# A two-layer trunk with a mixture of experts: the second layer's out projection taken tile by tile, late rows normed on VectorE, low weight parts behind the overflow branch

## The chip, the cores and the metric

The kernel runs on one core of one Trainium2 chip. The metric is the device time of one launch in microseconds; lower is better. TensorE (PE) multiplies matrices, VectorE (DVE) and ScalarE (ACT) do elementwise work, GpSimd (POOL) does elementwise work and issues the indirect (gathering) DMAs, SyncE (SP) issues the other DMAs.

## The reference

512 rows of 1024 numbers pass two layers. Layer 0 mixes by a chunked causal gMLP, layer 1 by dilated attention (three dilation groups of four heads); beside the mixer each layer attends to a memory of 256 rows. Then each layer does the same:

```
att = concat([mix, mo], -1) @ w_out            # out projection
x = layer_norm(ALPHA * x + att, ln1_g, ln1_b)
expert, gate = route(h, w_router, b_router)    # softmax, best group of 4 experts, top 2 in it
ffn = moe_ffn(h, expert, gate, w_gate, w_up, w_down)   # (silu(x@wg) * (x@wu)) @ wd
x = layer_norm(ALPHA * x + ffn, ln2_g, ln2_b)
```

All is float32; there are 16 experts with three 1024x1024 matrices each.

## The kernel before

The 512 rows lie in four tiles of 128 (t = 0 to 3), the 1024 columns in two halves of 512. A float32 product is made of three fp32r products: each operand is split into a high part (`wh`, `xh`, `ah`; ScalarE's cast) and a low part (`wl`, `xl`, `al`; VectorE's subtraction), and TensorE adds wh*xh, wl*xh and wh*xl.

**Recording and order.** The program is written once in Python and a scheduling layer of the framework sets the order on each engine, except in the expert stage, where the kernel's own generators do it (their helper is line 68). An engine's queue is in order: an instruction that waits holds all behind it.

**Out projection and first norm** (`out_proj_ln1`). The weights `woutb` are split one 128x1024 chunk of two half rows at a time, the tiles are taken in two pairs, and each pair splits all chunks again. For each (tile, half) the products collect in the PSUM tile `att`; VectorE adds it to `ALPHA` times the row (`xrows`, L770), takes statistics (L771), TensorE turns the rows (`hTp`), ScalarE copies them (`hT`), and TensorE makes the router's logits from them. Small steps on VectorE (L175 to L180, a Newton iteration for the reciprocal root; L787, L788) fix up the logits into `lg` (L794), so the router doesn't wait for the normed rows. The rows are normed beside: ScalarE (L793), then times `ln_g` (L797) and plus `ln_b` (L798) on GpSimd, with three of the eight L797 on VectorE; then each tile goes to `hbuf` in HBM. In layer 1 the products of the dilated attention's last group of heads (`dsc`, `dpt`, `po`) and the turn of its mix (`mixT`, `catb`) stand ahead; out-projection products are ready for the memory's part of the columns before, and stand between them on TensorE. Layer 0 has a `fill`: the projections of the memory for layer 1 (`pm`, `v`, `kT`), issued in two parts around the routing.

**Routing** (`route`). From `lg` a softmax (L825 to L835, result `pr`), the choice of group and experts, ranks by matmuls, and indices `ix` (L985).

**Experts** (`moe`, `stream`). An indirect DMA on GpSimd gathers the rows of each of the first two experts from `hbuf` by `ix` into `xg`. `gates` makes the gate weights on VectorE. The first three weight chunks are split (`wh` and `wl` from `wexp`). Then every engine reads a number of overflow blocks (`tabi`) and branches: with these inputs there is no overflow, and the branch skips its code (L1254 to L1257). Behind the branch `stream` turns the gathered rows (`xt`), splits them (`xh`, `xl`) and runs gate, up and down products (`pg`, `pu`, `pd`). Its lines in the profile are L68. Memory comes from pools that are opened and closed in order, so a tile of a later pool can lie on that of an earlier one and must wait until its last reader is done.

Of the kernel before, what the change touches and what calls it, by code (L numbers as in the profile page):

```python
# [11 lines left out]
F32 = mybir.dt.float32  # L12
# [5 lines left out]
OP = mybir.AluOpType  # L18
# [56 lines left out]
class Trunk:  # L75
# [106 lines left out]
    def rsqrt(self, pool, var):  # L182
        t = pool.tile([P, 3], F32, tag="rsq", name="rsq", bufs=2)
        list(self.rsqrt_steps(t, var, self.nc.vector))
        return t[:, 0:1]
# [557 lines left out]
    def out_proj_ln1(self, layer, spl, pl, wo, cat, order, xr, g, b, more, buf, fill=None):  # L743
# [6 lines left out]
        for pair in range(2):  # L750
            tiles = (2 * pair, 2 * pair + 1)
            accs = {(t, half): self.acc("att") for half in range(2) for t in tiles}
            st = {t: pl.tile([P, 2, 6], F32, tag="lst", name="lst", bufs=4) for t in tiles}
            hT = {t: pl.tile([P, KT, P], F32, tag="hT", name="hT", bufs=2) for t in tiles}
            for half in range(2):
                nj = nk // 2
                for js in [(j,) for j in range(nj - 2)] + ([(nj - 2, nj - 1)] if pair and half else [(nj - 2,), (nj - 1,)]):
                    parts = {j: self.split(spl, wo[half][:, order[2 * j]:order[2 * j] + 2]) for j in js}
                    for t in tiles:
                        ts = slice(t * P, (t + 1) * P)  # L760
                        for j in js:
                            h, l = parts[j]
                            for i in range(2):
                                c = slice(i * 512, (i + 1) * 512)
                                k = order[2 * j] + i
                                self.mm3(accs[t, half], (cat[k][0][:, ts], cat[k][1][:, ts]), (h[:, c], l[:, c]),
                                         start=(j == 0 and i == 0), stop=(j == nj - 1 and i == 1))
                for t in tiles:
                    z = xr[:, t, half * 512:(half + 1) * 512]
                    nc.vector.scalar_tensor_tensor(z, z, ALPHA, accs[t, half], op0=OP.mult, op1=OP.add)  # L770
                    nc.vector.bn_stats(st[t][:, half], z)  # L771
                    x = self.tp("hTp")
                    for i in range(4):
                        nc.tensor.transpose(x[:, i * P:(i + 1) * P], z[:, i * P:(i + 1) * P], self.ident)
                    nc.scalar.copy(hT[t][:, 4 * half:4 * half + 4].rearrange("p a b -> p (a b)"), x)
            if pair:
                self.early += [self.load_half(layer, *divmod(i, 6)) for i in more]
                if not fill:
                    for t in range(2):
                        nc.sync.dma_start(self.hbuf[t * P:(t + 1) * P, :], xr[:, t])  # L780
                self.table(pl, AF.Exp, lg[:, 1, :1])
            for t in tiles:
                mv = pl.tile([P, 2], F32, tag="lmv", name="lmv", bufs=2)
                nc.vector.bn_aggr(mv, st[t])
                rs = self.rsqrt(pl, mv[:, 1:2])
                sh = pl.tile([P, 1 + NE], F32, tag="lsh", name="lsh", bufs=2)
                nc.vector.scalar_tensor_tensor(sh[:, :1], mv[:, 0:1], -1.0, rs, op0=OP.mult, op1=OP.mult)  # L787
                nc.vector.scalar_tensor_tensor(sh[:, 1:], sums[:, 0], sh[:, :1], sums[:, 1], op0=OP.mult, op1=OP.add)  # L788
                o = lps[t % 2][:, t * NE:(t + 1) * NE]
                for k in range(KT):  # L790
                    last = nc.tensor.matmul(o, hT[t][:, k], gw[:, k], start=(k == 0), stop=(k == KT - 1))
                z = xr[:, t]
                nc.scalar.activation(z, z, AF.Identity, scale=rs, bias=sh[:, :1])  # L793
                nc.vector.scalar_tensor_tensor(lg[:, t], o, rs, sh[:, 1:], op0=OP.mult, op1=OP.add)  # L794
                for half in range(2):
                    v = slice(half * 512, (half + 1) * 512)
                    (nc.vector if t + half > 2 else nc.gpsimd).tensor_mul(z[:, v], z[:, v], g[:, v])  # L797
                nc.gpsimd.tensor_add(z, z, b)  # L798
                if pair or fill:
                    nc.sync.dma_start(self.hbuf[t * P:(t + 1) * P, :], z)  # L800
        if fill:
            with self.tc.issue_after(last.ins):
                fill(0)
        self.route(Carve(buf()), lg)
# [14 lines left out]
    def route(self, pl, lg):  # L819
# [205 lines left out]
    def wh_tile(self, pool):  # L1025
        return pool.tile([P, 1024], F32R, tag="wh", name="wh", bufs=AHEAD_H + 1)
# [90 lines left out]
    def stream(self, layer, px, pool, scat, loaded, chunk, parts):  # L1117
# [29 lines left out]
        for _ in rows_in(0):  # L1147
            pass
# [285 lines left out]
```

## Time and profile before

| | us |
|---|---|
| median of 3 runs | 1694.1 (1692.45 to 1694.6) |
| profiled execution | 1693.88 |
| its span, first to last instruction | 1692.0 |
| TensorE busy | 1585.1 (94%) |
| VectorE busy | 1409.3 (83%) |
| ScalarE busy | 1136.5 (67%) |
| GpSimd busy | 228.2 (13%) |

Layer 0 lies up to about 200 us before its routing, its expert stage from 233 us to 780; layer 1's mixers and out projection end near 1067, its expert stage runs from 1089 to 1640. Times in rows count from the start of the span. A busy share is an average over all of these.

### The profile page before, as it was taken

What the parts mean: (1) busy time and instruction counts of PE and PEld (TensorE: products, weight loads), DVE (VectorE), ACT (ScalarE), POOL (GpSimd) and SP (SyncE); (2) the same over time, 40 slices, a digit from 0 to 9 for tenths busy, and PEclk for the clock granted to TensorE, in tenths of its full rate; (3) what the DMA queues carried; (4) which work ended last, traced back from release to release, by engine and by line L of the source; (5) the groups of instructions that cost most, each with busy time, mean ns of one, the idle gap of its engine ahead of it and who ended that gap; (6) DMA issues with size and microseconds to landing.
All of it is one profiled execution on the core that took longest, in us unless ns stands there. A gap on an engine that the chain in (4) does not pass through costs nothing. (4 is left out here: it accounts for less than half of the span.)

```text
span 1692.0 us, 21506 instructions
## 1 busy us (share of the span) xinstructions
PE 1585.1 (94%) x7608; PEld 1279.8 (76%) x7608; DVE 1409.3 (83%) x1934; ACT 1136.5 (67%) x1447; POOL 228.2 (13%) x159
## 2 busy tenths in 40 slices
PE   7999879999999999999599998499999999999994
PEld 6778768888888888886487787388888888888873
DVE  3856779999999999997735557899999999999998
ACT  3644458888888888885334434388888888888871
POOL 1201500000000000004500000300000000000035
PEclk9999989999999999999799998699999999999998
DMA  8516569999999999978331152599999999999951
GB/s 344 218 50 249 199 250 397 365 380 377 367 377 370 385 379 379 373 298 351 120 130 57 63 225 82 212 361 379 376 365 375 379 374 381 372 377 377 374 200 50
DMA packets 52165, 496.39 MB, mean 293 GB/s; under 512 B 10181, under 2 KB 10309, under 8 KB 22288
## 3 DMA queue, kind: packets, MB, share of 16 engines
q1 hardware_dynamic: 40560, 457.83, 69.2%
q0 software_dynamic: 10912, 35.00, 5.4%
q10 hardware_dynamic: 576, 2.10, 0.3%
q8 instruction: 62, 1.02, 0.2%
q14 instruction: 55, 0.45, 0.1%
HBM read 479.86 MB, written 34.64 MB: 304 GB/s over the span
## 5 line engine op out<-in xcount | busy, mean ns | idle before, releaser
L68 DVE TENSOR_TENSOR wl<-wexp,wh 128x1024 fp32r<-128x1024 f32 x762 | 928.1, 1242 | 38.1 <-ACT wh L68 9.4
L68 ACT ACTIVATE wh<-wexp 128x1024 fp32r<-128x1024 f32 x762 | 797.7, 1059 | 134.2 <-PE pg L68 57.7
L68 PE MATMUL pd<-wh,ah 128*128 128x512 f32 x512 | 210.5, 411 | 0.0
L68 PE MATMUL pd<-wl,ah 128*128 128x512 f32 x512 | 204.0, 398 | 4.7 <-DVE wl L68 4.7
L68 PE MATMUL pg<-wh,xh 128*128 128x512 f32 x512 | 204.3, 399 | 0.0
L68 PE MATMUL pd<-wh,al 128*128 128x512 f32 x512 | 203.1, 397 | 0.0
L68 PE MATMUL pu<-wh,xh 128*128 128x512 f32 x512 | 202.4, 395 | 0.0
L68 PE MATMUL pg<-wh,xl 128*128 128x512 f32 x512 | 200.5, 392 | 0.0
L68 PE MATMUL pg<-wl,xh 128*128 128x512 f32 x512 | 200.4, 391 | 0.0
L68 PE MATMUL pu<-wl,xh 128*128 128x512 f32 x512 | 199.7, 390 | 0.0
L68 PE MATMUL pu<-wh,xl 128*128 128x512 f32 x512 | 199.2, 389 | 0.0
L68 PEld LDWEIGHTS pd<-wl,ah 128*128 128x128 f32 x512 | 96.6, 189 | 29.3 <-DVE wl L68 6.4
L1001 POOL DMA_INDIRECT xg<-hbuf,ix x32 | 42.0, 1313 | 566.1 <-PE pu L68 482.1
L68 PEld LDWEIGHTS pg<-wl,xh 128*128 128x128 f32 x512 | 96.7, 189 | 21.0
L68 PEld LDWEIGHTS pd<-wh,al 128*128 128x128 f32 x512 | 97.1, 190 | 20.0 <-DVE al L68 0.2
L68 PEld LDWEIGHTS pg<-wh,xl 128*128 128x128 f32 x512 | 96.9, 189 | 20.1 <-DVE xl L68 0.9
L68 PEld LDWEIGHTS pg<-wh,xh 128*128 128x128 f32 x512 | 96.8, 189 | 19.6 <-issue 0.3
L68 PEld LDWEIGHTS pu<-wl,xh 128*128 128x128 f32 x512 | 96.1, 188 | 20.4
L68 PEld LDWEIGHTS pd<-wh,ah 128*128 128x128 f32 x512 | 97.0, 189 | 18.9
L68 PEld LDWEIGHTS pu<-wh,xl 128*128 128x128 f32 x512 | 96.2, 188 | 19.0
L68 PEld LDWEIGHTS pu<-wh,xh 128*128 128x128 f32 x512 | 96.1, 188 | 18.8
L1005 POOL DMA_INDIRECT ybuf<-y,ix x30 | 38.5, 1283 | 449.4 <-ACT y L68 449.4
(371 smaller groups left out, 2312.1 us busy)
## 6 DMA issues: line engine op xcount, KB each, us to landing
wexp<-w_moe SPq DMA_DIRECT2D x177, 2048.0 KB, 9.2
wexp<-w_moe SPq DMA_DIRECT2D x24, 1024.0 KB, 7.8
yrows<-ybuf SPq DMA_DIRECT2D x8, 1024.0 KB, 7.9
wb<-wbr SPq DMA_DIRECT2D x4, 2048.0 KB, 9.7
wexp<-w_moe POOLq DMA_DIRECT2D x3, 2048.0 KB, 10.0
ybuf<-mematt POOLq DMA_DIRECT2D x4, 1024.0 KB, 14.2
wina<-wina SPq DMA_DIRECT2D x2, 2048.0 KB, 19.4
wouta<-w_out_a SPq DMA_DIRECT2D x2, 2048.0 KB, 10.7
```

The costliest lines, as they stand in the source:

```text
L68: r = getattr(self.eng, name)(*args, **kw)
L1001: return self.nc.gpsimd.indirect_dma_start(out=xg, out_offset=None, in_=self.hbuf, in_offset=off, bounds_check=S - 1, oob_is_err=False)
L1005: st = self.nc.gpsimd.indirect_dma_start(out=self.ybuf, out_offset=bass.IndirectOffsetOnAxis(ap=ix[:, 1], axis=0), in_=y, in_offset=None, ...
```

## The change

It has four parts. (1) In layer 1, which has no `fill`, the out projection goes tile by tile, both halves of a tile one after the other; the four splits are made once and kept (those of the second half in another pool), and a tile's last turn, logits and rows are made in the middle of the next tile's products (`finish`). (2) The rows of tiles 2 and 3 are normed by two instructions of VectorE each, `(z - mean) * g` and `z * rs + b`, 1024 wide; in layer 0 and for layer 1's last tile they stand in the routing, behind the subtraction of the maximum (`between`). Tiles 0 and 1 have ScalarE and GpSimd as before, all of their products on GpSimd, the sum in two halves. (3) The casts of the first three weight chunks are no longer tied behind the gates; their subtractions stand behind the branch, two ahead of `xl` and one behind. (4) The `wh` tiles of the expert stage get a pool of their own (`pw`), opened first, so that all that follows lies at other addresses, `xg` too.

```diff
-        nk = len(order)
+        nj = len(order) // 2
...
-            for half in range(2):
-                nj = nk // 2
-                for js in [(j,) for j in range(nj - 2)] + ([(nj - 2, nj - 1)] if pair and half else [(nj - 2,), (nj - 1,)]):
-                    parts = {j: self.split(spl, wo[half][:, order[2 * j]:order[2 * j] + 2]) for j in js}
...
+        accs, st, hT, parts, norms = {}, {}, {}, {}, {}
+
+        def part(half, j, keep):
+            if (half, j) not in parts:
+                pool, bufs = (pl, 2) if keep and half else (spl, 2)
+                parts[half, j] = self.split(pool, wo[half][:, order[2 * j]:order[2 * j] + 2], bufs=bufs)
+            return parts[half, j] if keep else parts.pop((half, j))
...
+        def rows(t, eng=None):
+            mv, rs, sh = norms[t]
+            z = xr[:, t]
+            if eng:
                 nc.scalar.activation(z, z, AF.Identity, scale=rs, bias=sh[:, :1])
-                nc.vector.scalar_tensor_tensor(lg[:, t], o, rs, sh[:, 1:], op0=OP.mult, op1=OP.add)
                 for half in range(2):
                     v = slice(half * 512, (half + 1) * 512)
-                    (nc.vector if t + half > 2 else nc.gpsimd).tensor_mul(z[:, v], z[:, v], g[:, v])
-                nc.gpsimd.tensor_add(z, z, b)
-                if pair or fill:
-                    nc.sync.dma_start(self.hbuf[t * P:(t + 1) * P, :], z)
+                    eng.tensor_mul(z[:, v], z[:, v], g[:, v])
+                    eng.tensor_add(z[:, v], z[:, v], b[:, v])
+            else:
+                nc.vector.scalar_tensor_tensor(z, z, mv[:, 0:1], g, op0=OP.subtract, op1=OP.mult)
+                nc.vector.scalar_tensor_tensor(z, z, rs, b, op0=OP.mult, op1=OP.add)
+        def store(t):
+            nc.sync.dma_start(self.hbuf[t * P:(t + 1) * P, :], xr[:, t])
...
+            late = (2, 3)
+        else:
+            def finish(t):
+                turn(t, 1)
+                logits(t)
+                if t < 2:
+                    rows(t, nc.gpsimd)
+                elif t == 2:
+                    self.early += [self.load_half(layer, *divmod(i, 6)) for i in more]
+                    for i in range(2):
+                        store(i)
+                    rows(t)
+                    store(t)
+                    self.table(pl, AF.Exp, lg[:, 1, :1])
+
+            for t in range(NT):
+                for half in range(2):
+                    for j in range(nj):
+                        product(t, half, j, part(half, j, True))
+                    add(t, half)
+                    if t and half == 0:
+                        finish(t - 1)
+                    if half == 0:
+                        turn(t, 0)
+                stats(t)
+            finish(NT - 1)
+            late = (3,)
+
+        def between():
+            for t in late:
+                rows(t)
+                store(t)
+
+        self.route(Carve(buf()), lg, between)
...
-        nc.vector.tensor_sub(z, lg, mx[:, :, None].to_broadcast(TE))
+        sub = nc.vector.tensor_sub(z, lg, mx[:, :, None].to_broadcast(TE))
         pe = tl(TE)
         nc.scalar.activation(pe, z, AF.Exp)
         silu = self.table(pl, AF.Silu, pe[:, 0, :1])
+        with self.tc.issue_after(sub.ins):
+            between()
...
-    def wh_tile(self, pool):
-        return pool.tile([P, 1024], F32R, tag="wh", name="wh", bufs=AHEAD_H + 1)
+    def wh_tile(self):
+        return self.pw.tile([P, 1024], F32R, tag="wh", name="wh", bufs=AHEAD_H + 1)
...
-        with tc.tile_pool(name=f"moe_x{layer}", bufs=1) as px, tc.tile_pool(name=f"moe{layer}", bufs=1) as pool:
+        with ExitStack() as es:
+            self.pw, px, pool = (es.enter_context(tc.tile_pool(name=f"moe_{n}{layer}", bufs=1)) for n in "wxp")
...
-            with tc.issue_after(self.gated.ins), tc.issue_after(self.counted.ins):
-                for k, p in enumerate(parts):
-                    self.split_to(chunk(k), *p)
+            for k, p in enumerate(parts):
+                nc.scalar.activation(p[0], chunk(k), AF.Copy)
...
+        for k, p in enumerate(parts):
+            if k < 2:
+                self.dve.tensor_sub(p[1], chunk(k), p[0].bitcast(F32))
         xs = []
         for _ in rows_in(0):
             pass
+        for k, p in enumerate(parts):
+            if k >= 2:
+                self.dve.tensor_sub(p[1], chunk(k), p[0].bitcast(F32))
```

The order of instructions below is without time. On TensorE, in layer 1 at the end of the dilated attention (`po`, `dpt`: its last heads; `mixT`: the turn of its mixed result, one per tile; `att`: out-projection products), before:

```order
L693 MATMUL po<-vs,mp 128x64 x4
L123 MATMUL att<-wh,catb 128x512 x3
L724 MATMUL mixT<-ident,oall 128x128 x2
L687 MATMUL dpt<-ident,mp 128x128 x4
L123 MATMUL att<-wl,catb 128x512
L123 MATMUL att<-wh,catb 128x512
L687 MATMUL dpt<-ident,mp 128x128 x4
L123 MATMUL att<-wh,catb 128x512
L693 MATMUL po<-vs,mp 128x64 x8
L123 MATMUL att<-wl,catb 128x512
```

and now:

```order
L724 MATMUL mixT<-ident,oall 128x128 x2
L687 MATMUL dpt<-ident,mp 128x128 x4
L693 MATMUL po<-vs,mp 128x64 x4
L687 MATMUL dpt<-ident,mp 128x128 x4
L693 MATMUL po<-vs,mp 128x64 x4
L724 MATMUL mixT<-ident,oall 128x128 x2
L780 MATMUL hTp<-ident,xrows 128x128 x4
L738 MATMUL gbw<-gbp,onesf 128x32
L796 MATMUL logits<-gbw,hT 128x16 x4
L123 MATMUL att<-wh,catb 128x512 x2
L123 MATMUL att<-wl,catb 128x512
```

The products no longer stand between the heads: of the 96 `att` products of layer 1, 65 stood ahead of the last `mixT` before, and 12 stand there now.

On VectorE, in layer 1's routing from the maximum to the softmax's result `pr`, before:

```order
L825 TENSOR_REDUCE rt<-lg 128x4
L827 TENSOR_TENSOR rt<-lg,rt 128x64
L797 TENSOR_TENSOR xrows<-xrows,ln_g 128x512 x3
L832 TENSOR_REDUCE rt<-rt 128x4
L833 RECIPROCAL rt<-rt 128x4
L835 TENSOR_TENSOR pr<-rt 128x64
```

and now:

```order
L893 TENSOR_REDUCE rt<-lg 128x4
L895 TENSOR_TENSOR rt<-lg,rt 128x64
L810 SCALAR_TENSOR_TENSOR xrows<-xrows,lmv,ln_g 128x1024
L902 TENSOR_REDUCE rt<-rt 128x4
L811 SCALAR_TENSOR_TENSOR xrows<-xrows,rsq,ln_b 128x1024
L903 RECIPROCAL rt<-rt 128x4
L905 TENSOR_TENSOR pr<-rt 128x64
```

The last tile's two row instructions (four in layer 0, for two tiles) have taken the place of the multiplications by `ln_g`.

On GpSimd, in layer 0 at the start of the expert stage (`xg`: the gathers; the branch is the third row, its skipped code is left out between the two pieces), before:

```order
L1001 DMA xg_1824<-hbuf,ix 128x1024
L1254 TENSOR_LOAD tabi
L1255 COMPARE_AND_BRANCH
```

```order
L1255 UNCONDITIONAL_BRANCH
L1001 DMA xg_1825<-hbuf,ix 128x1024
L1021 DMA wexp<-w_moe 128x4096 x2
```

and now:

```order
L1071 DMA xg_1825<-hbuf,ix 128x1024
L1071 DMA xg_1826<-hbuf,ix 128x1024
L1091 DMA wexp<-w_moe 128x4096 x2
L1330 TENSOR_LOAD tabi
L1331 COMPARE_AND_BRANCH
```

Both gathers and the two weight loads now stand ahead of the branch.

## Rows read from the trace of the kernel before

**Rows 1.** Stretches of the span, busy time of each engine with the count of its instructions, granted TensorE clock, share of the DMA engines and GB/s.
```profile
230.00:600.00 370.00, 369.25 (x1727) 301.52 (x1728) 347.32 (x369) 302.83 (x337) 26.13 (x20) 0.99 0.97 380
1000.00:1040.00 40.00, 34.78 (x173) 25.31 (x172) 30.68 (x88) 17.06 (x51) 1.42 (x2) 0.96 0.28 113
1100.00:1640.00 540.00, 540.00 (x2533) 441.66 (x2532) 510.00 (x535) 444.87 (x495) 39.99 (x30) 1.00 0.93 366
```

**Rows 2.** The chain that ended last, at the start of layer 1's expert stage (start, length, engine, tile, line, count).
```profile
1091.34 4.81 PE pg L68 x12
```

**Rows 3.** Timeline of layer 0 between the last logits and the top-2 selection, first VectorE, then GpSimd (start, length, engine, line, operation, output<-inputs, shapes, count; in brackets the idle time ahead and what ended it).
```profile
200.73 0.69 DVE L797 TENSOR_TENSOR xrows<-xrows,ln_g 128x512 f32<-128x512 f32 x1
201.84 0.79 DVE L827 TENSOR_TENSOR rt<-lg,rt 128x64 f32<-128x64 f32 x1
202.56 3.48 DVE L797 TENSOR_TENSOR xrows<-xrows,ln_g 128x512 f32<-128x512 f32 x2
206.42 2.22 DVE L835 TENSOR_TENSOR pr<-rt 128x64 f32<-128x64 f32 x1
...
206.21 2.35 POOL L798 TENSOR_TENSOR xrows<-xrows,ln_b 128x1024 f32<-128x1024 f32 x1 [0.72 <-DVE rt L832]
```

**Rows 4.** Timeline of layer 0 at the end of the routing and the start of the expert stage: TensorE, GpSimd, ScalarE.
```profile
225.11 0.44 PE L223 MATMUL kT<-ident,kT 128*128 128x128 f32 x2 [0.52 <-ACT kT L221]
230.75 1.94 PE L68 MATMUL xt<-ident,xg 128*128 128x128 f32 x8 [5.20 <-DMA xg<-hbuf,ix]
232.57 0.80 PE L68 MATMUL pg<-wh,xh 128*128 128x512 f32 x1
...
225.32 1.10 POOL L1001 DMA_INDIRECT xg<-hbuf,ix  x1 [16.76 <-ACT kT L221]
227.51 1.01 POOL L1001 DMA_INDIRECT xg<-hbuf,ix  x1 [1.08 <-remote]
...
225.65 0.58 ACT L224 COPY kT<-kT 128x512 f32<-128x512 f32 x1 [0.59 <-PE kT L223]
231.93 0.60 ACT L68 ACTIVATE xh<-xt 128x512 fp32r<-128x512 f32 x1 [5.69 <-PE xt L68]
```

**Rows 5.** Timeline of layer 1 through the last dilated tiles and the start of its out projection: TensorE, then VectorE and ScalarE.
```profile
1031.90 0.41 PE L724 MATMUL mixT<-ident,oall 128*128 128x128 f32 x2 [2.21 <-DVE mixw L709]
1040.13 0.40 PE L123 MATMUL att<-wl,catb 128*128 128x512 f32 x1
1040.36 0.62 PE L123 MATMUL att<-wh,catb 128*128 128x512 f32 x2
1041.05 0.38 PE L724 MATMUL mixT<-ident,oall 128*128 128x128 f32 x2
1041.27 0.60 PE L774 MATMUL hTp<-ident,xrows 128*128 128x128 f32 x4
1047.17 1.86 PE L791 MATMUL logits<-gbw,hT 128*128 128x16 f32 x16
...
1032.42 1.22 DVE L119 TENSOR_TENSOR wl<-woutb,wh 128x1024 fp32r<-128x1024 f32 x1
1043.72 0.57 DVE L736 TENSOR_REDUCE gbp<-gbw 128x32 f32<-128x256 f32 x1
...
1040.15 1.06 ACT L118 ACTIVATE wh<-woutb 128x1024 fp32r<-128x1024 f32 x1 [1.35 <-PE att L123]
```

**Rows 6.** Granted TensorE clock in three stretches around the same work (columns as in rows 1).
```profile
1029.00:1032.00 3.00, 0.80 (x4) 0.35 (x4) 2.61 (x8) 2.84 (x9) 0.00 (x0) 1.00 0.00 0
1032.00:1035.00 3.00, 2.05 (x10) 1.51 (x11) 3.00 (x7) 0.91 (x5) 0.00 (x0) 0.77 0.01 3
1065.00:1095.00 30.00, 6.68 (x38) 5.15 (x39) 26.06 (x89) 11.26 (x14) 9.13 (x7) 0.50 0.48 180
```

**Rows 7.** Timeline of layer 1 from the last product of the out projection to the last logits: TensorE, VectorE, GpSimd.
```profile
1058.19 0.39 PE L123 MATMUL att<-wh,catb 128*128 128x512 f32 x1
...
1057.28 0.69 DVE L770 SCALAR_TENSOR_TENSOR xrows<-xrows,att 128x512 f32<-128x512 f32 x1 [5.53 <-PE att L123]
1062.97 2.19 DVE L179 SCALAR_TENSOR_TENSOR rsq<-rsq 128x1 f32<-128x1 f32 x1
1067.33 0.23 DVE L794 SCALAR_TENSOR_TENSOR lg<-logits,rsq,lsh 128x16 f32<-128x16 f32 x1
...
1062.80 2.34 POOL L798 TENSOR_TENSOR xrows<-xrows,ln_b 128x1024 f32<-128x1024 f32 x1
```

**Rows 8.** Timeline of layer 1's routing and the start of its expert stage, VectorE, GpSimd, VectorE again, TensorE; the last line is from the view of DMA issues of the same stretch (count, median us from issue to landing).
```profile
1067.85 1.31 DVE L827 TENSOR_TENSOR rt<-lg,rt 128x64 f32<-128x64 f32 x1
1069.08 4.03 DVE L797 TENSOR_TENSOR xrows<-xrows,ln_g 128x512 f32<-128x512 f32 x3
1073.49 2.21 DVE L835 TENSOR_TENSOR pr<-rt 128x64 f32<-128x64 f32 x1
...
1082.94 1.11 POOL L1001 DMA_INDIRECT xg<-hbuf,ix  x1 [7.32 <-DVE ix L983]
...
1085.75 3.49 DVE L119 TENSOR_TENSOR wl<-wexp,wh 128x1024 fp32r<-128x1024 f32 x3
1089.40 1.94 PE L68 MATMUL xt<-ident,xg 128*128 128x128 f32 x8 [6.99 <-DVEq L1255]
...
xg<-hbuf,ix POOLq DMA_INDIRECT x2, 4.6
```

More of the change, by code (lines that the diff above doesn't have):

```diff
@@ L746, in out_proj_ln1 @@
         gw, sums = self.router_weights(layer, pl)
-        nk = len(order)
+        nj = len(order) // 2
         lg = pl.tile([P, NT, NE], F32, name="lg")
         lps = [self.sc("logits") for _ in range(2)]
[L750 to L754, printed above, removed]
-            for half in range(2):
-                nj = nk // 2
-                for js in [(j,) for j in range(nj - 2)] + ([(nj - 2, nj - 1)] if pair and half else [(nj - 2,), (nj - 1,)]):
-                    parts = {j: self.split(spl, wo[half][:, order[2 * j]:order[2 * j] + 2]) for j in js}
[L759 to L792, printed above, removed]
@@ new lines, in out_proj_ln1, with product @@
+        accs, st, hT, parts, norms = {}, {}, {}, {}, {}
[4 more added lines that the diff above has]
+            return parts[half, j] if keep else parts.pop((half, j))
+        def product(t, half, j, hl):
+            if j == 0:
+                accs[t, half] = self.acc("att")
+            ts = slice(t * P, (t + 1) * P)
+            for i in range(2):
+                c = slice(i * 512, (i + 1) * 512)
+                k = order[2 * j] + i
+                self.mm3(accs[t, half], (cat[k][0][:, ts], cat[k][1][:, ts]), (hl[0][:, c], hl[1][:, c]),
+                         start=(j == 0 and i == 0), stop=(j == nj - 1 and i == 1))
@@ new lines, in add, with turn @@
+        def add(t, half):
+            if half == 0:
+                st[t] = pl.tile([P, 2, 6], F32, tag="lst", name="lst", bufs=4)
+                hT[t] = pl.tile([P, KT, P], F32, tag="hT", name="hT", bufs=2)
+            z = xr[:, t, half * 512:(half + 1) * 512]
+            nc.vector.scalar_tensor_tensor(z, z, ALPHA, accs[t, half], op0=OP.mult, op1=OP.add)
+            nc.vector.bn_stats(st[t][:, half], z)
+        def turn(t, half):
+            z = xr[:, t, half * 512:(half + 1) * 512]
+            x = self.tp("hTp")
+            for i in range(4):
+                nc.tensor.transpose(x[:, i * P:(i + 1) * P], z[:, i * P:(i + 1) * P], self.ident)
+            nc.scalar.copy(hT[t][:, 4 * half:4 * half + 4].rearrange("p a b -> p (a b)"), x)
@@ L793, in out_proj_ln1, with logits @@
+        def logits(t):
+            mv, rs, sh = norms[t]
+            o = lps[t % 2][:, t * NE:(t + 1) * NE]
+            for k in range(KT):
+                self.mm = nc.tensor.matmul(o, hT[t][:, k], gw[:, k], start=(k == 0), stop=(k == KT - 1))
+            nc.vector.scalar_tensor_tensor(lg[:, t], o, rs, sh[:, 1:], op0=OP.mult, op1=OP.add)
+        def rows(t, eng=None):
+            mv, rs, sh = norms[t]
+            z = xr[:, t]
+            if eng:
                 nc.scalar.activation(z, z, AF.Identity, scale=rs, bias=sh[:, :1])
-                nc.vector.scalar_tensor_tensor(lg[:, t], o, rs, sh[:, 1:], op0=OP.mult, op1=OP.add)
```

43 lines of the change are left out of this document (36 added, 7 removed).

## The prediction

> **What bounds the kernel now.** The table of stretches comes first. In both expert stages TensorE is busy without a break: 369.25 of 370 us and 540.00 of 540 us at a granted clock of 0.99 and 1.00, with VectorE at 347 of 370 [rows 1]. The change leaves those matmuls as they are, so a stage takes as long as before and only the moment counts at which its first pg matmul starts. The second view, the chain that ended last, agrees: from the first pg of layer 1 on it runs through pg, pu and pd [rows 2]. The third view is the timeline ahead of those two moments: pg at 232.57 in layer 0 [rows 4], and xt at 1089.40 in layer 1, 1.94 us ahead of pg [rows 2, 8]. Everything below asks by how much these two move. The last dilated tiles of layer 1 lie ahead of the second; there VectorE is busy for 30.68 of 40 us and TensorE for 34.78, of which part is out-projection work that fills its waits [rows 1].
>
> **Layer 0, the router.** The reader is to see three things [rows 3]: L797 (0.69) stands ahead of the last lg; two more L797 take 3.48 inside the softmax; and pr (L835), 64 wide, takes 2.22, because it runs beside GpSimd's L798 of 2.35 and ends when that ends. The nearest rows to the new row instruction (1024 wide, both inputs in SBUF) are the subtractions of the same width: 1.22 alone, and three in 3.49, so 1.16 in a row [rows 5, 8]. Sum from the old start of the last lg: it is 0.5 earlier without L797 (200.8); 0.23 for it, two steps of 0.25 up to the subtraction (0.79 before, beside GpSimd's work), four row instructions 4.65, then reduction, reciprocal and pr at 0.2 to 0.25 each: pr ends near 206.9, where it ended at 208.64. That is **-1.7 us** for the selection and all that follows it.
>
> **Layer 0, the start of the experts.** Gather 1 issues at 225.32, when TensorE's last pm product lets go of the memory (its releaser is the kT copy behind it), and xt starts 5.4 us later, when the rows have landed [rows 4]. The indices were ready far earlier: GpSimd stood idle for 16.76 us ahead of the gather [rows 4]. With the pools laid out anew the gather waits for indices and stored rows alone; it issues near 214.3 and lands near 219.7, so the landing leaves the path. What is late next: TensorE's own kT turn, done at 225.55 before, now 223.85; and ScalarE, which gets one wh cast (1.06 [rows 5]) ahead of its last kT copy and two behind it. The copy ends near 225.0, the casts near 227.0. Then ScalarE takes its branch. The trace has no such branch with nothing to cover it except GpSimd's: 1.08 us between its two gathers [rows 4]; the lower bound is 0.1, an issue gap. With xh (0.60) and 0.1 to the first product, pg starts between 227.7 and 228.8; I take 228.3, so **-4.3 us**. The cover that is gone is worth naming: the gather's landing hid ScalarE's casts and branch.
>
> The Trainium skill, "Runtime: NRT & Kernel Launch", section "Instruction fetch mechanics", has a taken branch whose target lies outside the prefetched pages stop the engine for a fetch; GpSimd's 1.08 us agrees in kind. By that rule every engine pays at the branch that the low parts used to cover, and the sum would stand at its late end, pg at 228.8 and the time at 1689.7.
>
> Low parts behind the branch cost VectorE 2.3 us (two subtractions) before xl. They run while xt and xh do, so pg's first product waits for none of them; its second waits for xl at worst some tenths, paid once in each layer.
>
> **Layer 1, the last dilated tiles.** Of the 96 att products, 65 stood ahead of the last mixT; 12 do now. Four of the eight splits go with them, each 1.22 on VectorE and 1.06 on ScalarE [rows 5]. mixT of a tile waits for VectorE: 2.21 us idle at 1031.90 [rows 5]. Without two subtractions and with fewer adds a tile of 9.2 us (1031.90 to 1041.05) and the two longer ones ahead shorten by some 2.5 each, together 7 to 8, so the last mixT moves from 1041.05 to 1033 at full clock. But TensorE then works less: in the two stretches around 1032 it was busy for 0.80 of 3 us, and then the granted clock was 0.77 [rows 6]. I take 1035 (bounds 1030, if the chain of small operations alone counts, and 1041, if none of it does).
>
> **Layer 1, the out projection.** From mixT to the first product of the next half stand its copy, the router weights' products and reduction (0.57 the latter), one matmul, two copies and one cast (1.06): about 4.0 [rows 5]. Then 84 products, 0.23 apart (1040.13 to 1040.36), 19.4 us; six turns of four transposes at 0.36 (0.60 with the tail that the next instruction overlaps), 2.2; five sets of logits at 0.85 (16 records take 1.86), 4.3 [rows 5]: 25.8. I add 2.8, for about 14 products at half clock instead of full, as the routing stretch at 0.50 shows that clock after low activity [rows 6], and 1.0 for VectorE's steps beside GpSimd's rows of tiles 0 and 1. The last product ends near 1068.6; before it ended at 1058.58 [rows 7]. This part alone is **+10 us**.
>
> From there to the last lg were 9.0 us, 1058.58 to 1067.56, in which two tiles' statistics took turns and one Newton step of some 0.15 took 2.19, beside GpSimd's L798 of 2.34 [rows 7]. Now one tile is left: add and statistics 1.4 (0.69 each [rows 7]), fourteen dependent small steps 2.6, lg and its wait 0.6: 4.6, **-4.4**. From lg to the end of pr: before 8.1 (1067.56 to 1075.70, with L797 at 4.03, the subtraction at 1.31 and pr at 2.21 [rows 8]); now two row instructions 2.4 and six steps of 0.2 to 0.25: 3.7, **-4.4**. From pr to gather 1 nothing changes: 7.2 [rows 8]. Behind it xt waited for VectorE's branch, 6.99 us idle, which stood behind three subtractions of 3.49 ending at 1089.24 [rows 8]; in all 6.5 from the gather's start to xt. Now the gather's landing ends last, and this layer's two gathers land 4.6 after their issue, which stands some 0.3 behind the start of the row [rows 8]: 4.9, **-1.6**. In sum +10.0 - 4.4 - 4.4 - 1.6 = **-0.4 us** for layer 1.
>
> **Sum.** -4.3 - 0.4 = -4.7 against the profiled execution's own 1693.88 us (0.2 below the median of 1694.1): **1689.2 us**. A measurement of this kernel can tell about 0.2%, or 3.4 us, from no change.
>
> **The rivals.** (B) *The out projection runs unhindered*: no fall of the clock and no hold, last mixT at 1033. Then 2.8, 1.0 and 2.0 fall away: layer 1 at -6.2; with the smaller gain on VectorE (7 of 7 to 8) I put it at -5.2, the time at **1684.4**. For it speaks that a stretch with gaps kept 1.00 (1029 to 1032 [rows 6]); against it the next row.
>
> (C) *The clock stays low*: the products that filled TensorE's waits are gone, and the out projection now starts behind a thin stretch. If another 28 of the 84 products run at half clock, 0.2 us more each, layer 1 gets 5.6 later: +5.2, the time **1694.8**. The row at 0.77 behind a thin one speaks for it [rows 6]; against it, that the out projection itself keeps TensorE full.
>
> The Trainium skill, "TensorE: Matmul & The Clock Gate", section "HAM oscillation — how this bites in real kernels", says that bursts of matmuls with waits between them start cold again and again. This speaks against taking the filler out; the 0.77 agrees with it, and by it alone the time would be that of C.
>
> (D) *GpSimd's rows hold VectorE* (slower). Rows of tiles 0 and 1 are normed on GpSimd in the middle of the out projection, eight operations of about 1.2, 9.7 us together, and the Newton steps of the following tiles have two SBUF inputs, the kind that took 2.19 [rows 7]. If VectorE is held through all of it, each next tile's add is late, TensorE's accumulators stay full, and 8.7 come on top: 1689.2 + 8.7 = **1697.9**. It decides from about 8.5 held microseconds on; against it, L770 with one input in PSUM ran its usual 0.69 beside such work [rows 7].
>
> (E) *The new layout does nothing for gather 1* beyond the router's shift, since something else holds ScalarE or xg: layer 0 at -1.7, the time **1691.8**. For it: the releaser of the gather is inferred; against it: 16.76 us of idle time that no index explains [rows 4].
>
> **How the numbers follow.** Forecast 0.45 (its own range 1686.9 to 1691.4), B 0.17, C 0.17, D 0.11, E 0.10. The range that should hold 8 in 10 reaches from 1684.2 (B's middle; half of B beyond it) to 1697.2 (most of D beyond it). Faster by over 0.2% (below 1690.7): the forecast but for a small part, and B: 0.57. Within 0.2%: E, most of C, the rest of the forecast: 0.31. Slower: D and C's end: 0.12.
>
> **What would show it.** Right: in layer 0, gather 1 issues near 214, no GpSimd idle time is released by the kT copy, and pg starts near 228.3; in layer 1, mixT of the last tile is 6 earlier and the last att product some 10 later than before against the layer's start, pr keeps to 0.25 in both routers, and xt's releaser is the gather. Wrong: a granted clock near 0.5 through the att products (C); Newton steps of 1 us and more in the out projection (D); xt or xh waiting in layer 0 on something later than 228.8 (E); an expert stage whose length changes, which this working excludes altogether.

## The result and the profile after

The changed kernel takes 1705.63 us (median of 4 runs, 1704.62 to 1708.77) against 1694.14: a ratio of 1.0073, 95% interval 1.0055 to 1.0090. It is 12 us slower where 5 us less was forecast; the range ended at 1697.2. The span of its profiled execution is 1703.9 us, 11.9 longer.

Where the time lies, by six moments of the two timelines (us; dsc, dpt, po and mixT are the four products of a dilated tile, pg the first product and xt the first turn of an expert stage):

| | before | changed | difference |
|---|---|---|---|
| layer 0: first pg | 232.57 | 227.39 | -5.2 |
| layer 0 done: turns of layer 1's input (L511) | 821.25 | 817.80 | -3.5 |
| layer 1: first dsc of the last group | 998.44 | 996.48 | -2.0 |
| last mixT | 1041.05 | 1043.19 | +2.1 |
| end of the last att product | 1058.58 | 1080.00 | +21.4 |
| layer 1: first xt | 1089.40 | 1100.78 | +11.4 |

Layer 0 gains more than forecast. Its rows answer [rows 3, 4] (timeline of the changed kernel; VectorE, GpSimd, ScalarE, TensorE):

```profile
200.87 0.23 DVE L895 TENSOR_TENSOR rt<-lg,rt 128x64 f32<-128x64 f32 x1
201.01 2.48 DVE L810 SCALAR_TENSOR_TENSOR xrows<-xrows,lmv,ln_g 128x1024 f32<-128x1024 f32 x2
203.40 2.48 DVE L811 SCALAR_TENSOR_TENSOR xrows<-xrows,rsq,ln_b 128x1024 f32<-128x1024 f32 x2
206.26 0.23 DVE L905 TENSOR_TENSOR pr<-rt 128x64 f32<-128x64 f32 x1
...
214.61 1.29 POOL L1071 DMA_INDIRECT xg<-hbuf,ix  x1 [16.95 <-DVE ix L1055]
...
224.52 2.02 ACT L1183 ACTIVATE wh<-wexp 128x1024 fp32r<-128x1024 f32 x2
226.74 1.08 ACT L68 ACTIVATE xh<-xt 128x512 fp32r<-128x512 f32 x2 [0.20 <-ACTq L1331]
...
225.05 1.07 PE L68 MATMUL xt<-ident,xg 128*128 128x128 f32 x8 [1.35 <-PEq L1331]
227.39 0.79 PE L68 MATMUL pg<-wh,xh 128*128 128x512 f32 x1 [1.27 <-ACT xh L68]
```

The subtraction takes 0.23 and pr 0.23, gather 1 goes out at 214.61, released by the indices, and xt and pg start as soon as TensorE's own branch and ScalarE's casts are done.

Layer 1's attention is where the loss begins. These are stretches of 6 and of 2 us of the changed kernel (columns as in [rows 1]: length; TensorE, weight loads, VectorE, ScalarE, GpSimd busy; clock; DMA):

```profile
1002.00:1008.00 6.00, 4.79 (x12) 2.78 (x11) 3.42 (x11) 1.73 (x6) 0.00 (x0) 0.50 0.94 404
1012.00:1014.00 2.00, 2.00 (x15) 1.65 (x13) 0.53 (x4) 0.59 (x1) 0.00 (x0) 1.00 0.23 91
1014.00:1016.00 2.00, 2.00 (x13) 1.40 (x12) 0.98 (x3) 0.37 (x1) 0.00 (x0) 1.00 0.00 0
1020.00:1026.00 6.00, 5.22 (x17) 3.94 (x18) 3.08 (x11) 1.36 (x6) 0.39 (x1) 0.50 0.16 45
1038.00:1044.00 6.00, 2.95 (x13) 2.59 (x13) 1.89 (x4) 1.04 (x3) 0.00 (x0) 0.50 0.00 0
1044.00:1050.00 6.00, 4.38 (x17) 3.68 (x16) 3.95 (x7) 2.88 (x5) 0.00 (x0) 0.50 0.49 179
```

The granted clock is 0.50, which is 1.2 of 2.4 GHz, from 1002 to 1011 and from 1020 to 1050, although TensorE shows 3 to 5 us of work in 6. Between them it is 1.00: there the last 6 of the 12 out-projection products stand between the heads, from 1010.0 to 1015.9. In the kernel before, where they stood there throughout, it was 0.96 over 40 us [rows 1]. The timeline of TensorE shows what that does to the heads:

```profile
1022.68 2.07 PE L667 MATMUL dsc<-qks 64*128 64x256 f32 x4
1033.05 0.66 PE L724 MATMUL mixT<-ident,oall 128*128 128x128 f32 x2 [3.06 <-DVE mixw L708]
1043.19 0.69 PE L724 MATMUL mixT<-ident,oall 128*128 128x128 f32 x2 [2.37 <-DVE oall L720]
```

The same four dsc in the kernel before:

```profile
1024.20 1.13 PE L667 MATMUL dsc<-qks 64*128 64x256 f32 x4
```

They take 2.07 us at 0.50 against 1.13 at 1.00. The four products of a tile depend on one another, so each of them at half clock lengthens the chain; mixT then waits for VectorE (3.06 and 2.37 us), which waited for them.

In the out projection TensorE waits for rows between its products at two places, 1.23 and 1.01 us; the first (VectorE, GpSimd, TensorE):

```profile
1063.33 1.31 DVE L179 SCALAR_TENSOR_TENSOR rsq<-rsq 128x1 f32<-128x1 f32 x1
1064.68 1.20 DVE L180 SCALAR_TENSOR_TENSOR rsq<-rsq 128x1 f32<-128x1 f32 x1
1066.05 0.68 DVE L773 SCALAR_TENSOR_TENSOR xrows<-xrows,att 128x512 f32<-128x512 f32 x1
...
1063.36 2.50 POOL L808 TENSOR_TENSOR xrows<-xrows,ln_b 128x512 f32<-128x512 f32 x2
...
1066.78 0.33 PE L780 MATMUL hTp<-ident,xrows 128*128 128x128 f32 x1 [1.23 <-DVE xrows L773]
```

Two steps of the Newton iteration that take 0.16 to 0.22 alone take 1.31 and 1.20, until GpSimd's operations beside them end (two operations in 2.50 us); the add (L773) stands behind them, and TensorE's turn waits 1.23 for it.

The routing and the start of the experts answer [rows 7, 8]:

```profile
1084.20 0.23 DVE L797 SCALAR_TENSOR_TENSOR lg<-logits,rsq,lsh 128x16 f32<-128x16 f32 x1
1087.59 0.23 DVE L905 TENSOR_TENSOR pr<-rt 128x64 f32<-128x64 f32 x1
...
1095.89 1.11 POOL L1071 DMA_INDIRECT xg<-hbuf,ix  x1 [20.68 <-DVE scratch L978]
...
1100.78 1.94 PE L68 MATMUL xt<-ident,xg 128*128 128x128 f32 x8 [6.26 <-DMA xg<-hbuf,ix]
```

From the last product to lg 4.4, to the end of pr 3.4, to the gather 8.1, to xt 4.9: 20.8, where 30.8 stood before.

### The profile page after: what moved, and what is told of

It is laid out like the page before. It is cut to its first block, busy times and chain, and to the rows that moved or that the text cites. A ratio compares the mean times of both kernels' runs of the same rounds, so it can differ in the third digit from the quotient of the medians.

```text
span 1703.9 us, 21479 instructions
## 1 busy us (share of the span) xinstructions
PE 1591.7 (93%) x7608; PEld 1283.9 (75%) x7608; DVE 1406.4 (83%) x1932; ACT 1127.6 (66%) x1439; POOL 217.2 (13%) x157
## 4 chain that ended last, share of the span: by engine, by line
PE 45%; DVE 4%; issue 1%; DMA 0%; ACT 0%; ACTq 0%; DVEq 0%
PE pg L68 10%; PE pu L68 10%; PE pd L68 10%; PE qk L123 4%; PE va L123 2%; PE dsc L667 1%; PE po L693 1%; PE att L123 1%; PE xt L68 1%; PE at L68 1%; DVE wl L68 1%; DVE bnmv L68 1%; PE dpt L687 1%; PE msc L239 0%; PE mo L264 0%
## 5 line engine op out<-in xcount | busy, mean ns | idle before, releaser
L68 ACT ACTIVATE wh<-wexp 128x1024 fp32r<-128x1024 f32 x762 | 797.6, 1059 | 135.2 <-PE pg L68 60.0
```

The costliest lines, as they stand in the source:

```text
L68: r = getattr(self.eng, name)(*args, **kw)
```

## The experiments

Moments as in the table above, from each run's profiled execution; the ratio is that of the timed runs to the kernel before on the same chip. The runs lie on more than one chip, and the kernel before took 1694.1 to 1697.1 us there, so two runs are compared by their ratios. The column from dsc to the last mixT is called the phase below, the one from the last product to xt the tail. A product of the out projection that stands between the heads is a filler.

| run | ratio, 95% interval | first pg | dsc to last mixT | mixT to last product | to xt |
|---|---|---|---|---|---|
| before | 1 | 232.57 | 42.6 | 17.5 | 30.8 |
| changed | 1.0073 [1.0055, 1.0090] | 227.39 | 46.7 | 36.8 | 20.8 |
| e1 pairs again | 0.9954 [0.9941, 0.9968] | 226.96 | 44.8 | 14.3 | 29.8 |
| e3 dummy filler | 1.0003 [0.9994, 1.0013] | 228.26 | 37.9 | 36.0 | 21.1 |
| e8 rows on VectorE | 1.0043 [1.0028, 1.0058] | 226.88 | 46.7 | 34.1 | 22.2 |
| e11 = e1 + rows on VectorE | 0.9954 [0.9940, 0.9968] | 227.18 | 46.8 | 17.2 | 26.2 |
| e12 = e11 + warm start | 0.9968 [0.9956, 0.9980] | 229.86 | 46.8 | 15.6 | 28.6 |
| e13 = e1, old pools | 0.9948 [0.9933, 0.9962] | 231.54 | 44.9 | 14.3 | 29.6 |
| e14 = e1, low parts ahead | 0.9971 [0.9962, 0.9980] | 231.51 | 44.9 | 14.6 | 30.4 |
| e15 = e11 + filler | 0.9962 [0.9950, 0.9973] | 227.13 | 44.6 | 15.5 | 28.6 |
| e17 = e1, old rows | 1.0020 [1.0006, 1.0033] | 229.10 | 46.8 | 17.1 | 33.7 |
| e18 = before, no filler | 1.0083 [1.0061, 1.0105] | 231.90 | 47.9 | 32.0 | 28.7 |
| e19 half by half | 0.9986 [0.9975, 0.9998] | 226.87 | 44.1 | 21.9 | 26.7 |

**e1: the out projection in pairs again, the rest kept.** The loop of layer 0 serves both layers (where layer 1 stores its rows is left out here):

```diff
-        if fill:
+        if True:
             for tiles in ((0, 1), (2, 3)):
```

> The changed kernel with layer 1's out projection in two pairs of tiles again (eight splits, 65 of 96 products ahead of the last mixT); rows on VectorE, low parts behind the branch and the new pools stay. Theory 1 (the loss is the out projection taken tile by tile): the attention phase of layer 1 from its first dsc to the last mixT takes 42 to 43 us as in the kernel before (46.7 in the changed one), the clock there stays near 1.0, the last product comes some 17.5 us after the last mixT (36.8 in the changed one), and from it to xt 23 to 24 us pass (30.8 before, 20.8 changed, two more row instructions). Time 1684 to 1687 us. Theory 2 (the loss comes from row instructions or from the new addresses in layer 1): time stays at 1698 us or more.

Measured: 0.9954, 1.2% or some 20 us below the changed kernel. Part 1 is the loss; the other three parts together gain. But the tail is 29.8 and not 23 to 24, and the phase 44.8 and not 42 to 43. Stretches of its dilated attention:

```profile
1020.00:1026.00 6.00, 6.00 (x36) 4.55 (x34) 4.19 (x17) 2.73 (x7) 0.00 (x0) 1.00 0.20 48
1032.00:1038.00 6.00, 6.00 (x25) 5.59 (x24) 2.43 (x6) 0.96 (x2) 0.00 (x0) 0.50 0.00 0
```

The clock holds through three of the four tiles, as theory 1 said, and falls in the last, from about 1029 to 1039.

**e3: filler nobody reads, in the changed kernel.**

```diff
+            if g == 0:
+                dm = self.acc("dm")
+                for i in range(7):
+                    self.pe.matmul(dm, ch[:, 2 + s, bq], ch[:, 3], start=i == 0, stop=i == 6)
             x = self.tp("dpt")
```

> The changed kernel with 56 products added whose result nobody reads, of the shape of the out projection's, between the heads of the last dilated group of layer 1. Theory 1 (part of the loss is the clock, which fell to 0.50 once nothing filled TensorE's waits): the granted clock from the first dsc to the last mixT stays above 0.9, this phase falls from 46.7 to 37 to 41 us although TensorE has more to do, and the time falls to 1696 to 1700 us. Rival (the phase is longer for another reason, VectorE's or ScalarE's chain): the clock rises and the phase stays at 46 us or longer, the time at 1705 us or more.

```profile
1002.00:1008.00 6.00, 6.00 (x28) 4.01 (x28) 4.30 (x14) 2.08 (x9) 0.00 (x0) 1.00 1.01 434
1020.00:1026.00 6.00, 6.00 (x34) 4.50 (x33) 4.03 (x15) 1.23 (x5) 0.00 (x0) 1.00 0.18 48
```

56 products more, and the phase is 8.8 us shorter, at a clock of 1.00. The time falls by 0.7% to that of the kernel before. So the clock alone is worth some 9 us in this phase; nothing else was touched in it. It is not the whole loss against the forecast: with the clock held, the changed kernel is level with the one before and not 5 us faster.

**e18: the kernel before without its filler.** The reverse, in `out_proj_ln1` of the kernel before (`self.mixt` is the last turn of `mix_tile`):

```diff
-                                self.mm3(accs[t, half], ...
+                                with ExitStack() if fill else self.tc.issue_after(self.mixt.ins):
+                                    self.mm3(accs[t, half], ...
```

> The kernel before with one thing changed: no out-projection product of layer 1 may stand ahead of the last mixT (96 of 96 behind it, 31 before); pools, rows, low parts and the two pairs as before. Theory (without its filler the dilated attention lets the clock fall, whatever the rest): the granted clock from the first dsc to the last mixT falls to 0.5 to 0.7 in most of the phase, which gets no shorter than 42.6 us although 65 products have left it (44 to 48 us); the 65 products behind it cost 15 us at full clock; the time rises by 15 to 22 us to 1709 to 1716. Rival (only tile-by-tile order, pools or addresses slow the phase): the phase shortens to 35 us with those products gone, and the time rises by 8 us or less.

```profile
1002.00:1008.00 6.00, 3.97 (x10) 2.48 (x11) 3.62 (x14) 1.92 (x10) 0.00 (x0) 0.61 0.94 382
1020.00:1026.00 6.00, 4.75 (x14) 3.01 (x13) 3.46 (x9) 1.20 (x4) 0.00 (x0) 0.50 0.00 0
1038.00:1044.00 6.00, 4.31 (x18) 3.51 (x18) 4.10 (x16) 2.10 (x9) 0.00 (x0) 0.50 0.01 1
```

With pools, rows and order of before, the clock falls to 0.50 and the phase grows by 5.3 us although 65 products have left it; the products behind it, at full clock from about 1054 on, take 14.5 us more; the time rises by 0.8%, 14 us, a little less than the 15 to 22 expected. Both directions agree: the filler hid its own 15 us and kept the heads at full clock.

**e8: no GpSimd work in the out projection.**

```diff
                 if t < 2:
-                    rows(t, nc.gpsimd)
+                    rows(t)
```

> The changed kernel with the rows of tiles 0 and 1 of layer 1 also normed by two VectorE instructions each, so that GpSimd has nothing to do in the out projection. If GpSimd's work holds VectorE's Newton steps (1.31, 1.20, 1.08 and 1.21 us long in the changed kernel) and these make TensorE wait, the Newton steps go back to 0.22, the two holes of the out projection shrink, and the time falls by 2 to 4 us to 1702 to 1704. If the holes come from the order of the steps on VectorE and not from GpSimd, the two row instructions (1.28 each) take the holds' place and the time stays within 1 us of 1705.6 or gets worse.

```profile
1061.14 1.28 DVE L811 SCALAR_TENSOR_TENSOR xrows<-xrows,rsq,ln_b 128x1024 f32<-128x1024 f32 x1
1065.98 0.22 DVE L179 SCALAR_TENSOR_TENSOR rsq<-rsq 128x1 f32<-128x1 f32 x1
```

The Newton steps are back at 0.22 beside row instructions of 1.28, TensorE has no more holes between tiles, and the out projection is 2.7 us shorter (36.8 to 34.1). But the row instructions make the tail 1.4 us longer (22.2). The ratio is 0.3% below that of the changed kernel, and the two intervals just touch: the holds are real, and their 2.7 us are about a third of what the clock costs in the phase.

**e11: the same on the pairs.**

```diff
-                        rows(t, nc.gpsimd)
+                        rows(t, nc.gpsimd if fill else None)
```

In e1 the last pair's Newton steps are held again and again (VectorE of e1; x2 is two steps in one line):

```profile
1058.69 1.19 DVE L180 SCALAR_TENSOR_TENSOR rsq<-rsq 128x1 f32<-128x1 f32 x1
1059.81 2.52 DVE L179 SCALAR_TENSOR_TENSOR rsq<-rsq 128x1 f32<-128x1 f32 x2
1062.25 1.37 DVE L180 SCALAR_TENSOR_TENSOR rsq<-rsq 128x1 f32<-128x1 f32 x2
```

> The pairs of the first experiment, and the rows of tiles 0 and 1 of layer 1 normed on VectorE too (four more row instructions of 1.2 to 1.3 us there, no GpSimd work). Theory (GpSimd's rows hold the Newton steps of the last pair, 8.4 us from the last statistics to the first late lg where 3.5 would do): the time from the last product to xt falls from 29.8 to 25 to 26 us, as the four row instructions lie in VectorE's wait for the last products; 1684 to 1686 us. Rival (the row instructions push the last adds back by as much): 1688 us or more.

The tail falls from 29.8 to 26.2 as expected, but the timed runs are level with e1. In its profile the clock fell twice in the phase (near 1020 and from 1032 to 1042) and once in the out projection (1053 to 1059): the phase is 46.8 and the products take 17.2, 2.0 and 2.9 us more than in e1, and that gave the tail's gain back.

**e12: work on TensorE ahead of the experts**, on e11:

```diff
+        if layer:
+            self.warm(parts[0][0], 11)
         for _ in rows_in(0):
             pass
+        if not layer:
+            self.warm(parts[0][0], 8)
...
+    def warm(self, t, n):
+        dm = self.acc("dm")
+        for i in range(n):
+            self.pe.matmul(dm, t[:, :P], t[:, :512], start=i == 0, stop=i == n - 1)
```

> The kernel of the run before, with products whose result nobody reads on TensorE at the start of both expert stages: 8 behind the first xt of layer 0, 11 between the branch and the first xt of layer 1. Theory (the earlier start of layer 0 was partly given back, 5.2 to 3.5 us by the end of the stage, because TensorE idled ahead of it and ran its first 6 us at half clock): the clock in the first 6 us of both stages is 0.9 or more, layer 0's stage is 1 to 1.7 us shorter, layer 1's 2 to 3, and the time 2.5 to 4.5 us below the run before. Rival (what was given back went to the weights' transfers): the stages keep their length whatever the clock, same time within 1 us.

TensorE in layer 0, then layer 1's first stretches:

```profile
226.37 3.65 PE L68 MATMUL dm<-wh 128*128 128x512 f32 x8 [0.46 <-ACTq L1345]
229.86 0.39 PE L68 MATMUL pg<-wh,xh 128*128 128x512 f32 x1
...
1087.00:1090.00 3.00, 2.48 (x14) 1.76 (x13) 1.77 (x3) 2.40 (x4) 0.00 (x0) 1.00 0.79 333
1090.00:1093.00 3.00, 2.37 (x14) 1.64 (x13) 3.00 (x4) 2.58 (x3) 0.00 (x0) 1.00 0.18 49
```

The same stretches without it (e11):

```profile
1087.00:1090.00 3.00, 3.00 (x10) 2.14 (x9) 1.61 (x3) 2.15 (x4) 0.00 (x0) 0.50 0.98 404
```

In layer 0 the stage from pg to L511 takes 587.4 against 590.5, 3.1 less, half of the 6 us that e11 and the changed kernel spend at half clock; but pg starts 2.7 later, so 0.4 is left. In layer 1 the clock is 1.00 from the first pg, and the stage, to the end of its last pd, still takes 571.1 against 571.3: TensorE is now busy for only 2.48 and 2.37 of 3 us, and its waits there end on ScalarE's `xh` and VectorE's `xl` and `so`. The timed runs gain nothing (0.9968). The rival is right for layer 1.

**e13: the weight tiles back in the common pool, on e1.**

```diff
-            self.pw, px, pool = (es.enter_context(...) for n in "wxp")
+            px, pool = (es.enter_context(...) for n in "xp")
+            self.pw = pool
```

> The pairs of the first experiment with the weight tiles back in the common pool, as the kernel before had it. Theory (the new pools alone let layer 0's gather go ahead of the fill): gather 1 of layer 0 waits again for the kT copies, pg starts at 231 to 232 us instead of 227, with the router's 1.9 us still gained; the time rises by 2 to 4 us to 1690 to 1692. Rival: pg stays near 227, the pools do nothing.

```profile
224.06 1.10 POOL L1076 DMA_INDIRECT xg<-hbuf,ix  x1 [26.31 <-ACT kT L221]
...
229.72 1.94 PE L68 MATMUL xt<-ident,xg 128*128 128x128 f32 x8 [5.34 <-DMA xg<-hbuf,ix]
```

The gather waits for the kT copy again and pg starts at 231.5. That is the mechanism, as predicted; but the timed runs (0.9948) show no loss against e1 (0.9954), where 2 to 4 us were expected; the profiled execution, the slowest of its four runs, is 4.6 longer. What the pools are worth in time stays open, between nothing and 4 us.

**e14: low parts ahead of the branch, on e1** (their two loops in `stream` are gone):

```diff
-            for k, p in enumerate(parts):
-                nc.scalar.activation(p[0], chunk(k), AF.Copy)
+            with tc.issue_after(self.gated.ins), tc.issue_after(self.counted.ins):
+                for k, p in enumerate(parts):
+                    self.split_to(chunk(k), *p)
```

> The pairs of the first experiment with casts and low parts of the first weight chunks back ahead of the branch, behind the gates. Theory: in layer 1 the three subtractions (3.5 us) end about as late as the gather lands, so xt starts 0 to 1 us later; in layer 0 they end near 222.6 and the casts no longer delay the last kT copy; together within 1.5 us of the first experiment (1687 to 1690). Rival (the branch is the price once nothing covers it): a gain of 1 us or more in both layers.

```profile
215.87 1.30 POOL L1076 DMA_INDIRECT xg<-hbuf,ix  x1 [16.95 <-DVE ix L1060]
...
229.68 1.94 PE L68 MATMUL xt<-ident,xg 128*128 128x128 f32 x8 [4.45 <-DVEq L1331]
```

The gather goes out early, but xt waits for VectorE's branch behind gates and subtractions: pg starts at 231.5, and the gain of the pools is blocked in layer 0. Neither the theory nor its rival had this. The ratio is 0.17% above e1's, within what the intervals leave open. For an early pg the moved low parts (e14) and the pools (e13) are both needed; that this shows in the time is not shown.

**e17: old rows, on e1.**

```diff
-                    eng.tensor_mul(z[:, v], z[:, v], g[:, v])
-                    eng.tensor_add(z[:, v], z[:, v], b[:, v])
+                    (nc.vector if t + half > 2 else nc.gpsimd).tensor_mul(z[:, v], z[:, v], g[:, v])
+                nc.gpsimd.tensor_add(z, z, b)
...
-            late = (2, 3)
+            late = ()
```

> The pairs of the first experiment with the rows of tiles 2 and 3 normed the old way in both layers (ScalarE, GpSimd, and three of the multiplications on VectorE). Theory: the routers get back what they lost before, pr again takes 2.2 us and stands 1.7 to 1.9 us later in layer 0; in layer 1 the row instructions (4.95 us) give way to multiplications of 4.0 and held steps, 1.5 to 3 us later; the time rises by 2 to 5 us to 1690.5 to 1693.5. Rival (GpSimd's work lies in waits anyway): same time within 1 us of 1688.6.

```profile
201.10 0.80 DVE L899 TENSOR_TENSOR rt<-lg,rt 128x64 f32<-128x64 f32 x1
201.83 3.44 DVE L807 TENSOR_TENSOR xrows<-xrows,ln_g 128x512 f32<-128x512 f32 x2
205.65 2.21 DVE L909 TENSOR_TENSOR pr<-rt 128x64 f32<-128x64 f32 x1
...
1090.60 1.74 POOL L1075 DMA_INDIRECT xg<-hbuf,ix  x1 [11.47 <-DVEq L1335]
```

The router of layer 0 is back at 0.80, 3.44 and 2.21, pg starts 2.1 us later than in e1, and 0.66% of the time is lost. Much of it has other causes: gather 1 of layer 1 came to stand behind the branch (1090.60, after 11.47 us of idle time), and 4.8 of the 11.3 us by which its xt is later than in e1 lie in the phase and the products, where its clock fell for longer. 2 to 5 us were expected; this run is an upper bound on what the row instructions are worth.

**e15: filler for the pairs**, on e11, ahead of `mix_tile` (`mmi` is the tile's last po):

```diff
+            if b:
+                dm = self.tp("dm")
+                with self.tc.issue_after(mmi.ins):
+                    for i in range(8):
+                        nc.tensor.matmul(dm, ch[:, 2, bq], ch[:, 3], start=i == 0, stop=i == 7)
             self.mix_tile(pb, b, oall, ch, cl)
```

> Pairs, all rows of layer 1 on VectorE (the second batch's first run), and 8 products whose result nobody reads behind the heads of each of the last three dilated tiles, where TensorE waits for the mix. Theory (the phase took 46.8 us in that run and 44.8 in the first one, with the same order of work, because the clock fell to 0.50 at about 1029 us): the clock stays above 0.9 and the phase falls to 39 to 43 us; the time falls by 3 to 6 us to 1683 to 1686. Rival (the added products delay the heads of the next tile by as much, 1.9 us each): phase 45 us or longer, time 1688 or more.

```profile
1016.00:1032.00 16.00, 16.00 (x82) 12.06 (x81) 13.01 (x34) 7.23 (x19) 0.71 (x1) 1.00 0.06 18
1032.00:1042.00 10.00, 9.48 (x53) 7.09 (x52) 7.60 (x20) 3.60 (x9) 0.00 (x0) 1.00 0.00 1
1050.00:1056.00 6.00, 6.00 (x21) 5.20 (x21) 5.13 (x18) 1.17 (x2) 0.00 (x0) 0.51 0.64 232
```

The clock holds at 1.00 to the last mixT, but the phase is 44.6 us and the timed runs gain nothing (0.9962): the rival is right, the added products stand ahead of the next tile's heads, 2.09 us in a row. And the clock then falls in the out projection, where TensorE is just as busy.

**e19: half by half**, on e8. 42 products can stand in the phase:

```diff
-            for t in range(NT):
-                for half in range(2):
-                    for j in range(nj):
-                        product(t, half, j, part(half, j, True))
+            for j in range(nj):
+                for t in range(NT):
+                    product(t, 0, j, part(0, j, True))
+            for t in range(NT):
+                add(t, 0)
+                turn(t, 0)
+            for t in range(NT):
+                for j in range(nj):
+                    product(t, 1, j, part(1, j, True))
```

> The changed kernel with the four splits kept, but the products taken half by half: half 0 of all four tiles first, then half 1 tile by tile (42 of 96 products ahead of the last mixT where the changed kernel has 12 and the pairs 65), all rows of layer 1 on VectorE. Theory (what costs is the filler taken out; keeping it saves the four kept splits as well): the clock stays near 1.0 through the first two dilated tiles and the phase takes 41 to 45 us; 54 products, five sets of logits and the gap of 4 to 5 us behind the last mixT take 20 to 24 us, the tail 21 to 23; the time comes to 1686 to 1691 us, close to the pairs and 14 to 19 us below the changed kernel. Rival (the price lies in the splits of the second half, which can start only behind the last dilated tile): 24 us or more behind the last mixT, 1694 us or more.

```profile
1014.00:1034.00 20.00, 16.95 (x55) 13.15 (x55) 11.79 (x36) 6.30 (x22) 0.71 (x1) 0.51 0.05 14
1034.00:1040.00 6.00, 2.97 (x19) 2.53 (x18) 3.25 (x9) 0.96 (x2) 0.00 (x0) 0.78 0.00 0
```

It is 0.6% better than e8 with 30 more products in the phase, and 0.3% behind the pairs. The phase of 44.1 us and the 21.9 behind it are as expected; the tail is 26.7 and not 21 to 23, and the time lies above the expected 1686 to 1691 (1693.0). 42 products don't hold the clock either. Not only their number counts: 28 of them stand ahead of 1008, where the clock is 1.00, and 14 in the 32 us behind.

## Why the prediction was wrong

Point by point, forecast against measured:

- *Layer 0, the router, -1.7*: pr ends at 206.49, 2.15 earlier. Right; a row instruction costs 1.2 to 1.28 and not 1.16, but the small steps cost less.
- *Layer 0, the start, -4.3*: -5.2. Right in its mechanism (gather at 214.61, nothing held) and a little short: ScalarE's branch cost about 0.2 behind its casts, not up to 1.1. TensorE's took 1.35, but ended ahead of ScalarE's casts.
- That this gain would arrive whole was taken from [rows 1], where TensorE is busy without a break, and a stage of another length was excluded; this is the first miss: 2.0 of 5.2 reach layer 1. 1.7 go in the stage: from pg on TensorE ran 6.0 us at half clock, where before it was 2.3. e1, with 3.2 us of it, loses 0.4 there, and e12, with none, gains 1.3 on the kernel before: in layer 0 the stage's length follows the low stretch by half of it. Why it was 6.0 us here and 3.2 in e1, with nearly the same waits ahead of pg, stays open. 1.5 more go between L511 and dsc, in code that did not change; kernels with the same code there differ by as much (177.2 to 179.9 us), and what decides it stays open.
- *The last dilated tiles, mixT at 1035*: this step failed. 36.6 us were forecast for the phase and 46.7 measured, 10.1 of the 16.5 us between forecast and result. 8.8 of them are the clock: e3, which holds it, takes 37.9. The remaining 1.3 are not explained; at full clock 34.6 were forecast, so the saving may have been set too high, but e3 also carries its 56 products. The clock was taken from a row of before at 0.77 for 3 us [rows 6] and charged with 2 us, as an accident; with the filler gone it was 0.50 in most of the phase.
- *The out projection, 33.6 us from mixT*: 36.8. The gap was 5.5 and not 4.0, as it ran at half clock too, and the held steps cost 2.7 (e8) where 1.0 was set.
- *Tail and routing, 20.4*: 20.8, term by term within 0.4 but for the way from pr to the gather (8.1, 7.2 forecast).

Sum of the misses: 2.3 + 10.1 + 3.2 + 0.4, and 0.5 behind xt: 16.5 (the timed difference is 16.4).

Rival C named the cause, the filler that is gone, but put it in the wrong place: its price was 28 products of the out projection at half clock, its chance 0.17, and its time 1694.8. All but the first ten or so of the out projection's products ran at 1.00, from about 1052 on; the low clock lay ahead of them, in the attention's own dependent steps. The Trainium skill, "TensorE: Matmul & The Clock Gate", section "HAM oscillation — how this bites in real kernels", has bursts of matmuls with waits between them start cold again and again. The trace agrees in kind, with 0.50 from 1020 to 1050; there the waits are for DMA, here for ScalarE and VectorE. Rival D was right in kind, at 2.7 of its 8.7 us.

So what became of the gain: layer 0's earlier start and layer 1's tail, 10 us shorter, are there, and for that tail part 1 takes 23 us: 4 in the phase instead of a gain of 6, 19 in products that used to cost nothing. Undone (e1), the other three parts make the kernel 0.46% faster than before. No run did clearly better than e1, e11 and e13, which can't be told apart.

## What to carry to other kernels

Before independent matmuls are taken out of a chain of dependent ones, count what TensorE would still do there: in this kernel the filler was free in time, and it kept the clock of the chain itself near 1.00. Price such a chain at both clock levels, and take the lower one as a case with a good chance, not as an accident, when the engine's busy time in it drops; a forecast of "fewer instructions" that leaves the clock out can have the wrong sign. And an earlier start is worth less than it looks if the stage behind it runs longer at the low clock: here that took 1.7 of 5.2 us.

## What was not expected of the hardware

With 65 products ahead of the last mixT in each, the phase took 42.6, 44.8 and 46.8 us (before, e1, e11), and the clock was at 0.50 for some 3, 10 and 14 us of it. In all three it fell in the last tile, where few products stand, 3, 6 and 3 from 1029 to 1038; in e15, which has 24 there with its added ones, it stayed at 1.00. Why the same order of work loses the clock for 3 us once and for 10 another time stays open. It fell to 0.50 in the out projection as well (before, e11, e15, between 1047 and 1059), in or behind a stretch of transposes and 16-column logits in which the profile shows TensorE busy without a break. A VectorE instruction with two inputs in SBUF ended with GpSimd's running operation again and again, five times in a row in e1 (1.1 to 1.3 us a step where 0.15 to 0.22 is usual), so that the chain from the last statistics to lg, 3.4 us in e11, became 8.4.
